# Rotary crosswise halves of q and k: plain transfers into a zeroed tile and a VectorE addition in place of adding transfers from GpSimd

## The chip, the cores and the metric

The kernel runs on one core of one Trainium2 chip. The metric is the device time of one execution in microseconds (us); lower is better. The figure for the kernel before is the median of three timed runs, 1119.79 us (1118.19 to 1121.5).

## The reference

A decoder trunk of two layers over 512 tokens of width 1024, batch 1, all in float32. Layer 0 mixes tokens by differential attention with 8 heads, layer 1 by a short gated causal convolution; each mixer is followed by an MLP with a squared ReLU (1024 to 4096 and back), and every sub-layer has an RMSNorm ahead and one behind.

The change concerns layer 0. Each head has two q vectors and two k vectors of 64 entries. The first 16 entries of each are rotated by position: with x1 the first 8, x2 the next 8, and c, s tables of cosine and sine by position,

```
rot = [x1*c - x2*s, x2*c + x1*s]        # entries 0..15; entries 16..63 pass unchanged
```

The rotated q is scaled by 1/8, scores are masked causally, each of the two softmaxes is taken, and the output of a head is (p0 - lambda*p1) @ v, normalised per head and multiplied by the output weights.

## The kernel before, in words

**Precision.** Every large product is three matmuls: a float32 operand is held as a rounded high part and the low remainder, and `mm3` (L65 to L69) adds high*high, high*low and low*high in PSUM. `split` (L197) makes the parts of a weight: ScalarE copies (L198), VectorE subtracts (L199).

**Layout.** q and k are held with features on the 128 partitions (two vectors of 64) and the 512 positions on the free axis, one head at a time. So the 8 entries that the rotation adds to another 8 lie on other partitions, and an engine that works partition by partition cannot add them; a transfer carries them over.

**Rotation (`rotate`, L372).** When a head's q or k projection is complete in PSUM (bank 0 for q, bank 1 for k), VectorE writes two products: `sw` with the sine table (L374) and `t1` with the cosine table (L376). The trace calls them sw_q, sw_k, t_q and t_k. Four transfers of 8 partitions each then add rows of `sw` into `t1` crosswise; GpSimd issues them (L380, L381), with addition in the transfer. Two deferred pieces follow: `high` (L389) has ScalarE round `t1` into `sw`'s place (L391) and SyncE issue moves of halves into a tile for q or k, four for q and two for k (`move`, L387); `low` (L396) has VectorE form the remainder (L399 for k, L401 for q) and SyncE issue two more moves.

**Order around it.** Work is written as a stream of small steps; a step of the filler stream is one `mm3` of 512 columns. A projection is 8 steps, so a rotation falls due every 8 steps and a head (q and k) every 16. `after(n, fn)` runs fn n steps later: before, `high` 3 or 4 steps after its rotation and `low` one more; for head 0 all after 2 steps. Attention of a head runs in units of 128 queries, 4 per head and 32 in all, interleaved with the filler steps at 4 steps per unit: scores (L468, L470), masked maximum (L476), exponentials (L483), mixing (L498 to L501), transposes (L508), values (L517), sums of squares (L520), the power on GpSimd (L525, L526), the norm factor and its product (L535, L537), transposes of the result (L549) and its split (L553, L554). The scores of a head come 12 steps after the rotation of its k. A planner in the framework then lays out each engine's instructions from this order and from its own estimate of when operands are ready; on the chip each engine runs its list strictly in order.

**Queues.** SyncE (SP) issues all weight loads and the moves. GpSimd issues only the rotation's transfers, between its small arithmetic (L525, L526), in order.

**Buffers.** `sw` and `t1` have two buffers each; a `t1` buffer is also what the normed output `on` (L537) takes.

**After the attention** come the rest of the output projection, the MLP of layer 0, the convolution layer and the second MLP, which the change does not touch.

Of the kernel before, what the change touches and what calls it, by code (L numbers as in the profile page):

```python
# [10 lines left out]
F32 = mybir.dt.float32  # L11
F32R = mybir.dt.float32r
AF = mybir.ActivationFunctionType
ALU = mybir.AluOpType
AX = mybir.AxisListType

P = 128
T = 512
# [23 lines left out]
def trunk(ctx: ExitStack, tc: tile.TileContext, x, xT, w_qk, w_v, w_o, w_in, w_out,  # L42
          w_up, w_down, rows, cols, lam4, rope, out):
    nc = tc.nc
    PE, ACT, DVE, POOL = nc.tensor, nc.scalar, nc.vector, nc.gpsimd
# [34 lines left out]
    def after(n, fn):  # L80
        due.append([n, fn])
# [197 lines left out]
    ap = attn.enter_context(tc.tile_pool(name="attn", bufs=2))  # L279
    ropes = ap.tile([P, 2, T], F32, name="ropes", bufs=1)  # L280

    def t512(pool, name, tag, bufs):
        return pool.tile([P, 512], F32, tag=tag, name=name, bufs=bufs)
# [83 lines left out]
    for t in q_lo:  # L367
        for c, other in ((0, slice(HD, P)), (1, slice(0, HD))):
            POOL.memset(t[other, c, :].bitcast(F32), 0.0)
    qk, oT = {}, {}  # L370

    def rotate(i, which, h, p):  # L372
        sw = t512(ap, f"sw_{which}{h}", "c", 2)
        DVE.tensor_tensor(sw, p, ropes[:, 1], op=ALU.mult)  # L374
        t1 = t512(ap, f"t1_{which}{h}", "d", 2)
        DVE.tensor_tensor(t1, p, ropes[:, 0], op=ALU.mult)  # L376

        n = HD // 8
        for c in (0, HD):
            POOL.dma_start(t1[c:c + n], sw[c + n:c + 2 * n], accum_op=ALU.add)  # L380
            POOL.dma_start(t1[c + n:c + 2 * n], sw[c:c + n], accum_op=ALU.add)  # L381
        both = ap.tile([P, 2, T], F32R, tag=which, name=f"{which}_{h}")
        hi, lo = sw.bitcast(F32R), t1.bitcast(F32R)
        top, bot = slice(0, HD), slice(HD, P)

        def move(o, a):
            nc.sync.dma_start(o.bitcast(F32), a)  # L387

        def high():  # L389

            ACT.activation(hi, t1, AF.Copy, scale=1.0 if i else -HD ** -0.5)  # L391
            for c, mine, other in ((0, top, bot), (1, bot, top)):
                for o in (mine,) if i else (mine, other):
                    move(both[o, c, :], sw[mine])

        def low():  # L396

            if i:
                DVE.tensor_tensor(lo, t1, sw, op=ALU.subtract)  # L399
            else:  # L400
                DVE.scalar_tensor_tensor(lo, t1, -HD ** -0.5, sw, op0=ALU.mult, op1=ALU.subtract)  # L401
            for c, mine, other in ((0, top, bot), (1, bot, top)):
                move(both[other, c, :] if i else q_lo[h % 2][mine, c, :], t1[mine])
            qk[which, h] = both

        for fn, n in ((high, 3 if i else 4), (low, 4 if i else 5)):
            after(n if h else 2, fn)

    def projections():

        for h in range(H):
            for i, which in enumerate("qk"):
                w = use(which, h, lead=1)
                p = banks[i]
                for kt in range(KT):
                    yield lambda: mm3(p, part(w, ALL, slice(kt * P, (kt + 1) * P)), part(hT, ALL, kt),
                                      kt == 0, kt == KT - 1)
                done(which, h)
                rotate(i, which, h, p)
# [470 lines left out]
```

## Time and profile before

| | before |
|---|---|
| timed runs, median (lowest to highest) | 1119.79 us (1118.19 to 1121.5) |
| the profiled execution, its own time | 1123.18 us |
| its span in the trace | 1121.4 us |
| TensorE (PE) busy | 1094.6 us, 98% |
| VectorE (DVE) busy | 786.1 us, 70% |
| ScalarE (ACT) busy | 534.1 us, 48% |
| GpSimd (POOL) busy | 109.6 us, 10% |
| mean granted TensorE clock | 0.994 |

All times of rows are microseconds from the start of the span unless marked ns. A busy share is that of a whole span or stretch. PEld is the load of weights into TensorE, which runs beside its matmuls; SP is SyncE, and a "q" behind an engine's name is its sequencer. A wait is the idle time of an engine just before an instruction, put down to what ended last. The projections of head 0 end at about 56 us, the attention and the filler stream with it run from there to about 235 us, and the rest of the span is the layers after it.

### The profile page before, as it was taken

To read this page: it belongs to the slowest core of one execution; us is meant where nothing else is said; L and a number is where in the kernel's file an instruction comes from. 1 tells how busy PE (TensorE), PEld (TensorE's weight loads), DVE (VectorE), ACT (ScalarE), POOL (GpSimd) and SP (SyncE) were. 2 spreads that over 40 slices of the span, in tenths; PEclk is the share of its full clock that TensorE was granted. 3 is DMA by queue.
4 is the path that set the end of the run, shared out by engine and by line. 5 is a ranking of instruction groups with operands and counts; after the bars stand their busy time and mean duration, and the time that the engine had idled before them with its cause. 6 is when DMAs were issued, how large, how long until landed. Compare 5 with 4: busy or idle time off the path is not lost.

```text
span 1121.4 us, 14617 instructions
## 1 busy us (share of the span) xinstructions
PE 1094.6 (98%) x5404; PEld 921.2 (82%) x5404; DVE 786.1 (70%) x1235; ACT 534.1 (48%) x909; POOL 109.6 (10%) x177
## 2 busy tenths in 40 slices
PE   9999999999999999999998999999999999999997
PEld 8877777779888888888888988888988888888886
DVE  6557777655979778878687544346587887797766
ACT  6536565544754554554544422225375445445532
POOL 1145554211000000000001000000000000000000
PEclk9999999999999999999998999999999999999999
DMA  8665545135134314314043323213242242143202
GB/s 307 224 155 135 139 115 132 43 130 209 38 113 150 108 44 149 132 48 159 6 145 113 114 96 101 102 40 126 82 146 65 91 151 93 58 151 106 83 19 75
DMA packets 41495, 125.88 MB, mean 112 GB/s; under 512 B 6608, under 2 KB 7248, under 8 KB 41424
## 3 DMA queue, kind: packets, MB, share of 16 engines
q1 hardware_dynamic: 39232, 123.88, 33.7%
q0 software_dynamic: 2048, 1.06, 0.8%
q8 instruction: 42, 0.69, 0.3%
q14 instruction: 29, 0.24, 0.1%
q10 hardware_dynamic: 144, 0.02, 0.0%
HBM read 111.30 MB, written 2.10 MB: 101 GB/s over the span
## 4 chain that ended last, share of the span: by engine, by line
PE 75%; DVE 4%; issue 2%; POOL 2%; DMA 2%; ACT 2%; POOLq 0%; ACTq 0%; DVEq 0%
PE bank L69 24%; PE bank L68 24%; PE bank L67 24%; DMA t_k<-sw_k 1%; DVE x_sb L616 1%; PE bank L633 1%; DMA t_q<-sw_q 1%; PE pair L67 1%; PE pair L69 1%; PE pair L68 1%; DVE mg_m L611 0%; PE bank L517 0%; DVE acc L772 0%; ACT p L483 0%; DVE hn_m L625 0%
## 5 line engine op out<-in xcount | busy, mean ns | idle before, releaser
L67 PE MATMUL bank<-hT_hi,hi_up 128*128 128x512 f32 (+1 forms) x608 | 216.5, 356 | 0.0
L69 PE MATMUL bank<-hT_hi,lo_up 128*128 128x512 f32 (+1 forms) x608 | 216.2, 356 | 0.0
L68 PE MATMUL bank<-hT_lo,hi_up 128*128 128x512 f32 (+1 forms) x608 | 216.1, 355 | 0.0
L68 PEld LDWEIGHTS bank<-hT_lo,hi_up 128*128 128x128 f32 x608 | 114.9, 189 | 16.4
L67 PEld LDWEIGHTS bank<-hT_hi,hi_up 128*128 128x128 f32 x608 | 114.9, 189 | 16.3
L69 PEld LDWEIGHTS bank<-hT_hi,lo_up 128*128 128x128 f32 x608 | 114.9, 189 | 16.1
L728 DVE TENSOR_TENSOR acc<-acc,bank 128x512 f32<-128x512 f32 x180 | 116.7, 680 | 4.4 <-PE bank L69 4.4
L198 ACT CAST hi_up<-raw_up 128x1024 fp32r<-128x1024 f32 x64 | 67.2, 1054 | 87.5 <-PE bank L69 76.4
L199 DVE TENSOR_TENSOR lo_up<-raw_up,hi_up 128x1024 fp32r<-128x1024 f32 x64 | 76.7, 1218 | 8.4 <-ACT hi_up L198 8.4
L199 DVE TENSOR_TENSOR lo_G<-rawd,hi_G 128x1024 fp32r<-128x1024 f32 x28 | 34.2, 1221 | 44.2 <-ACT hi_G L198 44.2
L68 PE MATMUL bank<-hT_lo,hi_ci 128*128 128x512 f32 (+1 forms) x176 | 62.9, 358 | 1.8 <-DVE b_m L605 1.8
L67 PE MATMUL bank<-hT_hi,hi_ci 128*128 128x512 f32 (+1 forms) x176 | 62.8, 357 | 0.9 <-ACT hT_hi L636 0.8
L69 PE MATMUL bank<-hT_hi,lo_ci 128*128 128x512 f32 (+1 forms) x176 | 62.8, 357 | 0.0
L678 ACT ACTIVATE F<-bank 128x512 f32<-128x512 f32 x64 | 37.6, 594 | 45.2 <-PE bank L69 36.0
L198 ACT CAST hi_G<-rawd 128x1024 fp32r<-128x1024 f32 x28 | 29.5, 1054 | 46.2 <-PE bank L68 31.1
L199 DVE TENSOR_TENSOR lo_E<-rawd,hi_E 128x1024 fp32r<-128x1024 f32 x28 | 34.2, 1220 | 23.6 <-ACT hi_E L198 23.6
L199 DVE TENSOR_TENSOR lo_A<-rawd,hi_A 128x1024 fp32r<-128x1024 f32 x28 | 33.5, 1220 | 19.5 <-ACT hi_A L198 19.5
L483 ACT ACTIVATE p<-pair,nm 128x128 f32<-128x128 f32 (+3 forms) x64 | 33.1, 524 | 26.9 <-DVE nm L476 24.3
L198 ACT CAST hi_E<-rawd 128x1024 fp32r<-128x1024 f32 x28 | 29.3, 1048 | 34.8 <-PE bank L68 33.6
L67 PE MATMUL bank<-hi_A,ua_hi 128*128 128x512 f32 x112 | 44.1, 393 | 0.0
L198 ACT CAST hi_A<-rawd 128x1024 fp32r<-128x1024 f32 x28 | 29.5, 1054 | 30.3 <-PE bank L68 17.7
L68 PE MATMUL bank<-lo_A,ua_hi 128*128 128x512 f32 x112 | 43.6, 390 | 0.0
(303 smaller groups left out, 2663.0 us busy)
## 6 DMA issues: line engine op xcount, KB each, us to landing
raw_up<-in_w_up SPq DMA_DIRECT2D x64, 512.0 KB, 4.2
rawd<-in_w_down SPq DMA_DIRECT2D x56, 512.0 KB, 4.4
raw_ci<-in_w_in SPq DMA_DIRECT2D x24, 512.0 KB, 3.5
raw_q<-in_w_qk SPq DMA_DIRECT2D x8, 512.0 KB, 4.9
raw_k<-in_w_qk SPq DMA_DIRECT2D x8, 512.0 KB, 4.4
q<-sw_q SPq DMA_DIRECT2D x32, 128.0 KB, 2.4
raw_wo<-in_w_o SPq DMA_DIRECT2D x8, 512.0 KB, 3.6
raw_dn<-in_w_down SPq DMA_DIRECT2D x8, 512.0 KB, 3.4
```

Of the source, the lines that this page charges most:

```text
L67: PE.matmul(o, lhsT=a[0], rhs=b[0], start=start, stop=False, skip_group_check=more)
L68: PE.matmul(o, lhsT=a[0], rhs=b[1], start=False, stop=False, skip_group_check=more)
L69: PE.matmul(o, lhsT=a[1], rhs=b[0], start=False, stop=stop, skip_group_check=more)
L198: (DVE.tensor_copy if on_dve else ACT.copy)(hi, src)
L199: DVE.tensor_tensor(lo, src, hi.bitcast(F32), op=ALU.subtract)
L483: ACT.activation(p[:, c, :w], s[:, c, :w], AF.Exp, scale=-1.0, bias=nm[:, c:c + 1], accum_out=sums[:, c:c + 1])
L616: DVE.scalar_tensor_tensor(xn, m, r, xn, op0=ALU.mult, op1=ALU.add)
L633: PE.transpose(tp[:, j * P:(j + 1) * P], hns[n][:, j * P:(j + 1) * P], ident)
L678: ACT.activation(dst, o, AF.Relu)
L728: DVE.tensor_tensor(a, a, o[t], op=op)
```

## The change

Before the loop a tile `cross` of 128 by 512 float32 is allocated once and set to zero by GpSimd. In `rotate` the four transfers become plain copies, issued by SyncE, from `sw` into the rows of `cross` that correspond to the entries 0 to 15 of each vector; all other rows of `cross` stay zero for good. A new deferred piece `turned` has VectorE add `cross` to `t1`. It runs 6 steps after the rotation, `high` 7 and `low` 8 (head 0: all after 2 steps, as before). Since there is one `cross` tile, the copies of a rotation wait until the addition of the rotation before has read it.

```
+    cross = ap.tile([P, T], F32, name="cross", bufs=1)
+    POOL.memset(cross, 0.0)
     qk, oT = {}, {}

     def rotate(i, which, h, p):
...
         for c in (0, HD):
-            POOL.dma_start(t1[c:c + n], sw[c + n:c + 2 * n], accum_op=ALU.add)
-            POOL.dma_start(t1[c + n:c + 2 * n], sw[c:c + n], accum_op=ALU.add)
+            nc.sync.dma_start(cross[c:c + n], sw[c + n:c + 2 * n])
+            nc.sync.dma_start(cross[c + n:c + 2 * n], sw[c:c + n])
...
-        for fn, n in ((high, 3 if i else 4), (low, 4 if i else 5)):
+        def turned():
+            DVE.tensor_tensor(t1, t1, cross, op=ALU.add)
+
+        for fn, n in ((turned, 6), (high, 7), (low, 8)):
             after(n if h else 2, fn)
```

## Rows read from the trace of the kernel before

**Rows 1.** The page's first part: busy time, share, instructions.

```profile
PE 1094.6 (98%) x5404; PEld 921.2 (82%) x5404; DVE 786.1 (70%) x1235; ACT 534.1 (48%) x909; POOL 109.6 (10%) x177
```

**Rows 2.** Busy time by stretch: stretch, length, busy by engine (instructions), clock, DMA share, GB/s.

```profile
62.00:215.00 153.00, 140.09 (x744) 114.70 (x743) 110.88 (x304) 82.68 (x253) 75.12 (x116) 0.99 0.51 128
215.00:235.00 20.00, 20.00 (x105) 16.64 (x105) 6.78 (x22) 6.48 (x20) 3.16 (x8) 1.00 0.16 55
```

**Rows 3.** Waits, 62 to 215: who for whom, total, times, longest.

```profile
ACT sw_q L391 <- DMA t_q<-sw_q: 7.8, 5, 5.4
DVE t_q L401 <- ACT sw_q L391: 7.8, 6, 2.7
...
DVE f L535 <- POOL f L526: 7.0, 6, 1.6
PE pair L549 <- DVE on L537: 5.2, 5, 1.6
...
PE pair L468 <- ACT p L483: 2.5, 1, 2.5
```

**Rows 4.** The chain of waits, 139 to 185: start, length, what.

```profile
152.07 0.68 DVE sw_k L374
...
155.64 4.70 DMA t_k<-sw_k
...
172.51 0.68 DVE sw_k L374
```

**Rows 5.** Timelines of POOL, DVE, PE: start, length, instruction, [idle before, releaser].

```profile
155.64 1.67 POOL L381 DMA_DIRECT2D t_k<-sw_k  x1
157.38 0.23 POOL L525 TENSOR_SCALAR f<-ss 128x1 f32<-128x1 f32 x1
...
158.29 0.16 DVE L535 TENSOR_TENSOR f<-f,rc 128x4 f32<-128x4 f32 x1 [1.47 <-POOL f L526]
...
159.68 0.63 PE L549 MATMUL pair<-ident,on 128*128 128x128 f32 x4 [1.44 <-DVE on L537]
```

**Rows 6.** Timelines of PE and ACT around three waits of TensorE.

```profile
73.84 0.47 PE L468 MATMUL pair<-k,q 128*128 128x256 f32 x2 [0.24 <-DMA k<-t_k]
...
78.40 0.63 ACT L391 ACTIVATE sw_q<-t_q 128x512 fp32r<-128x512 f32 x1 [5.39 <-DMA t_q<-sw_q]
...
79.78 0.61 PE L468 MATMUL pair<-k,q 128*128 128x384 f32 x2 [2.45 <-ACT p L483]
...
129.55 0.63 ACT L391 ACTIVATE sw_q<-t_q 128x512 fp32r<-128x512 f32 x1 [2.04 <-issue]
...
131.62 0.66 PE L508 MATMUL bank<-ident,a 128*128 128x128 f32 x4 [2.14 <-DVE a L501]
```

**Rows 7.** Busy time by stretch, after the last of these waits (clock third from last).

```profile
132.00:134.00 2.00, 2.00 (x11) 1.69 (x10) 2.00 (x9) 1.29 (x5) 0.00 (x0) 0.67 0.87 203
134.00:136.00 2.00, 2.00 (x9) 1.81 (x9) 1.82 (x4) 0.94 (x5) 1.80 (x4) 0.50 0.60 127
```

**Rows 8.** Timeline of DVE: a remainder of k and the instruction behind it.

```profile
161.34 0.69 DVE L399 TENSOR_TENSOR t_k<-t_k,sw_k 128x512 fp32r<-128x512 f32 x1
161.95 0.74 DVE L554 SCALAR_TENSOR_TENSOR oT_lo<-pair,g_sub,oT_hi 128x512 fp32r<-128x512 f32 x1
```

**Rows 9.** SyncE: timeline of moves, then landing of q's transfers, then the k loads.

```profile
171.89 2.39 SPq L387 DMA_DIRECT2D q<-sw_q  x4
174.46 1.10 SPq L387 DMA_DIRECT2D q_lo<-t_q  x2
...
DMA to landing us min/median/max: 2.2/2.4/3.8
...
raw_k<-in_w_qk SPq DMA_DIRECT2D x8, 512.0 KB, 4.4
```

**Rows 10.** Timeline of POOL: zeroing at the start and the next work.

```profile
1.89 0.52 POOL L369 MEMSET q_lo<- 64x512 f32 x1
...
33.87 1.04 POOL L74 TENSOR_TENSOR r<-r,mhalf 128x4 f32<-128x4 f32 x1 [29.50 <-DVE r L73]
```

## The prediction

> **What bounds the kernel now.** I read the page's busy times first. TensorE is busy 1094.6 us of 1121.4 [rows 1], so a change elsewhere can only win back its idle time. The table of stretches says where that idle time is. From 62 to 215 us, where the rotations run beside the attention, TensorE is busy 140.09 of 153.00 us, so it idles 12.91 us; from 215 to 235 us, when the last rotation is done, it idles nowhere [rows 2]. 12.91 us is what this stage has to give.
>
> The chain of waits says what the stage waits for. From 139 us to the last rotation it hardly touches TensorE: it runs from VectorE's `sw` and `t1` through GpSimd's issue and the landing of the adding transfer to ScalarE's `high`, VectorE's `low` and the next `sw`. From one `sw_k` to the next it takes 172.51 - 152.07 = 20.44 us, and 4.70 us of it is one transfer of t_k underway [rows 4]. At 16 steps per head a step is 20.44 / 16 = 1.28 us.
>
> The timelines tell how this reaches TensorE, in two ways.
>
> First, through GpSimd. The last adding transfer of t_k was issued at 155.64 us and held GpSimd's sequence for 1.67 us; the small factor `f` behind it started only at 157.38, VectorE stood 1.47 us for it, and TensorE 1.44 us for the `on` that VectorE made with it [rows 5]. In the list of waits this is 7.0 us of VectorE in 6 waits, and 5.2 us of TensorE in 5 waits for `on` [rows 3].
>
> Second, through ScalarE. `high` stands in ScalarE's queue until its transfer has landed, and exponentials are queued behind it. At 78.40 us ScalarE had stood 5.39 us for t_q, and TensorE stood 2.45 us for the exponentials that came next; at 129.55 `high` was late again, VectorE's `low` waited for it with a mixing product queued behind, and TensorE stood 2.14 us for that product [rows 6]. In sum ScalarE stood 7.8 us for t_q, and VectorE's `low` of q as long for ScalarE [rows 3]. After the 2.14 us wait the granted clock was 0.67 and then 0.50, its lower level of 1.2 GHz, for two stretches of 2 us each [rows 7]; that costs (0.33 + 0.50) x 2 = 1.7 us.
>
> **The change part by part.** Removed: 64 issues on GpSimd, and with them both ways above. TensorE's waits for `on` (5.2), for the exponentials (2.5) and for the product (2.1) come to 9.8 of the 12.91 us, and with the clock's 1.7 us the gross gain is 11.5 us. `f` is then late only if the sum of squares on ScalarE is; ScalarE meets `high` when the data has been added for a step already.
>
> Added on VectorE: 16 additions of 128x512. No row shows this addition; the nearest is L399, also two SBUF operands of that size, 0.69 us long, with the next instruction starting 0.61 us behind it [rows 8]. 16 x 0.61 = 9.8 us of VectorE, or 16 x 0.69 = 11.0 by whole durations. VectorE is busy 110.88 of 153.00 us there [rows 2], so it has room, and it loses waits of 7.0 + 7.8 = 14.8 us. It becomes no bound, but its order is strict: the addition of k falls 6 steps, 7.3 us, after `sw_k`, which is where `f` and `on` are made: VectorE took up `f` 158.29 - 152.07 = 6.2 us after `sw_k`, and TensorE had `on` after 159.68 - 152.07 = 7.6 [rows 4, 5]. I charge half of these 8 additions to TensorE: 8 x 0.61 / 2 = 2.4 us. If all 16 were on the path it would be 9.8, if none, nothing.
>
> Added on SyncE: 64 issues. The moves of q cost 2.39 / 4 = 0.60 us each, the low ones 1.10 / 2 = 0.55 [rows 9]; the new ones have 8 partitions where these have 64, so 0.60 is the upper end, and nothing the lower. At 0.55 four are 2.2 us a rotation. The landing behind it is 2.2 to 3.8 us, 2.4 in the median, for moves on the same queue [rows 9]. For q, SyncE has just the two low moves of k ahead: 0.6 (`sw`) + 0.5 + 2.2 + 2.4 = 5.7 us after `sw_q` starts. For k it has the four and two moves of q ahead, 3.5 us from the end of `high`. With the gain a step is some 1.22 us; `high` starts one step ahead of `sw_k` and takes 0.63 [rows 6], so it ends 0.6 us ahead, and k lands at 3.5 - 0.6 + 2.2 + 2.4 = 7.5 us. The addition stands 6 steps, 7.3 us, behind `sw`: q lands 1.6 us early, k 0.2 us late. 8 x 0.2 = 1.6 us, of which I charge 1 us to TensorE; with a load in front, 3.8 - 2.4 = 1.4 us more for every k, it would be 8 x 1.6 = 13, and with SyncE free ahead of k nothing.
>
> The later `high` and `low`: the low moves of k now are issued behind step 8 and the two high ones, at about 11.5 us after `sw_k`, and land by 13.9; the scores stand 12 steps, 14.6 us, behind. That is covered by 0.7 us, and costs 1 us a head where it isn't.
>
> The first head: its pieces all come after 2 steps, its first scores waited 0.24 us for k already [rows 6]. A plain transfer lands 4.70 - 2.4 = 2.3 us sooner than the adding one [rows 4, 9], and the addition takes 0.6 of it: 1.7 us sooner if k's copies go ahead of q's six moves on SyncE, 3.5 - 1.7 = 1.8 us later behind them. I take 0.7 us, nearer to the second, since q's moves are written first.
>
> The zeroing of `cross` is twice the 0.52 us of half a tile, and GpSimd idles 29.50 us before its next work [rows 10]: nothing.
>
> **The sum.** -11.5 + 2.4 + 1.0 + 0.7 = -7.4, taken as -7 us. For the profiled execution, 1123.18 us, that is 1116; against the median of the timed runs, 3.4 us lower, 1119.79 - 7 = 1113 us.
>
> **A rule that speaks against it.** The row shows moves of SyncE landing within 3.8 us though 512 KB loads, 4.4 us in the median, share their queue [rows 9]. The Trainium skill, "DMA: Bandwidth & Descriptors", section "Queues, rings and completion order", says that each DMA engine takes the descriptors of one queue row in ring order, while different rows take turns. So a crosswise copy just behind a weight load on SyncE's row would wait for it, where GpSimd's row took turns. No row shows how often that will be; it is the mechanism of the slower rival below.
>
> **The rivals.**
> *Slower: VectorE waits for the copies.* Before, only ScalarE stood for a transfer; now VectorE does, with masks, mixing and weight remainders behind it. For: the k copies have hardly any margin. Against: the rows of landing, and that SyncE's six moves of q are 3.5 us of a head's 20. If each rotation's copies land 2.5 us later than worked out, behind loads and moves, q waits 0.9 us and k 2.7, 3.6 a head and 29 us in all; with two thirds of it reaching TensorE, -11.5 + 3.1 + 19 = +11, and with fewer such rotations less: I put the case at +5, 1125 us. It decides from a mean wait of about 0.8 us a rotation (16 x 0.8 x 2/3 = 8.4).
> *No change: the gaps close up and open elsewhere.* `on` also hangs on ScalarE's exponentials and squares, and the additions delay VectorE. If half of the gross gain comes, -5.7 + 4.1 = -1.6: 1118 us. A step that shrinks until k is late for the scores ends here too (7 heads x 1 us against 7).
> *More: all idle time goes.* 12.91 + 1.7 less 3 us of costs: -11.5, 1108 us. For it: nothing else in the stage is busier than VectorE's 72%. Against: the small waits for transposed products remain.
> *The order changes.* The planner lays out each engine anew; that can move TensorE's waits by a few us either way and is spread over the cases.
>
> **How the numbers follow.** Forecast (-4 to -10 us, 1110 to 1116): 0.45. More: 0.13. No change: 0.22. Slower: 0.20. A measurement can tell 0.3%, 3.4 us, from no change: faster 0.58, same 0.22, slower 0.20. The range that leaves out about a tenth on either side goes from 1106 to 1125.
>
> **What would show it.** Right: no wait of VectorE's L535 for GpSimd over 0.5 us, no ScalarE wait for a transfer at `high`, TensorE's idle time from 62 us to the last rotation down to about 6 us, the head's period at about 19.5 us, no stretch at 0.5 clock there. Wrong: waits of the new addition for the copies over 0.5 us in most heads, or scores waiting for k's low moves; the same idle time of TensorE under other names would be the second rival.

## The result, and the profile after

The changed kernel takes 1145.56 us (median; 1144.9 to 1147.31) against 1119.47 us (1118.19 to 1121.5) before: a ratio of 1.0234, interval 1.0214 to 1.0254, which is 26.2 us (24.0 to 28.4) slower where 7 us faster was forecast. Its profiled execution took 1144.9 us, with a span of 1143.1 us, 21.7 longer than that of before; that one lay 3.7 us above its median, so some 4 us of the difference don't show in the pair of traces.

First the page's busy times of the changed kernel.

```profile
PE 1103.3 (97%) x5404; PEld 926.0 (81%) x5404; DVE 798.0 (70%) x1251; ACT 534.1 (47%) x909; POOL 57.7 (5%) x114
```

Against [rows 1], TensorE runs the same 5404 instructions in 8.7 us more, and idles 1143.1 - 1103.3 = 39.8 us where it idled 26.8: 13.0 us more. The two make up the whole 21.7 us. VectorE's 16 additions are its 1251 - 1235 instructions more, and at 0.69 us each 11.0 of the 11.9 us more; GpSimd is rid of half its work. The stretches of the changed kernel (length, busy by engine, clock, DMA share, GB/s) say where it happened.

```profile
62.00:215.00 153.00, 135.25 (x672) 108.98 (x671) 110.03 (x282) 73.35 (x219) 22.95 (x48) 0.96 0.46 121
215.00:235.00 20.00, 13.86 (x64) 11.42 (x64) 10.53 (x34) 8.34 (x29) 3.66 (x8) 0.83 0.25 56
```

Beside [rows 2], TensorE's idle time is 17.75 us where it was 12.91, and 6.14 us where it was nothing, since the rotations now last past 215 us. The clock is 0.96 and 0.83 where it was 0.99 and 1.00; (0.99 - 0.96) x 153 + (1.00 - 0.83) x 20 = 8.0 us, most of the 8.7 us of longer matmuls. VectorE and ScalarE are busy for less of the stage than before: neither is the bound.

Next VectorE's and then SyncE's timeline of the changed kernel, one head of it (start, length, line, instruction).

```profile
137.85 0.69 DVE L376 TENSOR_TENSOR sw_k<-bank,ropes 128x512 f32<-128x512 f32 x1 [0.18 <-DMA k<-sw_k]
...
142.41 0.69 DVE L409 TENSOR_TENSOR t_q<-t_q,cross 128x512 f32<-128x512 f32 x1
...
149.72 0.69 DVE L376 TENSOR_TENSOR sw_q<-bank,ropes 128x512 f32<-128x512 f32 x1
...
153.96 0.68 DVE L409 TENSOR_TENSOR t_k<-t_k,cross 128x512 f32<-128x512 f32 x1
...
164.88 0.69 DVE L409 TENSOR_TENSOR t_q<-t_q,cross 128x512 f32<-128x512 f32 x1
```

```profile
143.13 0.64 SPq L382 DMA_DIRECT2D cross<-sw_k  x1
143.98 2.66 SPq L389 DMA_DIRECT2D q<-sw_q  x4
146.75 1.17 SPq L389 DMA_DIRECT2D q_lo<-t_q  x2
147.97 0.68 SPq L383 DMA_DIRECT2D cross<-sw_k  x1
148.71 0.68 SPq L382 DMA_DIRECT2D cross<-sw_k  x1
149.43 0.62 SPq L383 DMA_DIRECT2D cross<-sw_k  x1
...
154.66 0.65 SPq L382 DMA_DIRECT2D cross<-sw_q  x1
155.40 1.17 SPq L389 DMA_DIRECT2D k<-sw_k  x2
156.66 1.19 SPq L389 DMA_DIRECT2D k<-t_k  x2
157.90 0.68 SPq L383 DMA_DIRECT2D cross<-sw_q  x1
158.62 0.68 SPq L382 DMA_DIRECT2D cross<-sw_q  x1
159.34 0.62 SPq L383 DMA_DIRECT2D cross<-sw_q  x1
```

Read the two together. `sw_k` is done at 138.54, but its first copy is issued only at 143.13, at the moment the addition of q (142.41 to 143.10) has read `cross`: there is one `cross`, and k must not overwrite what q has not yet read. Behind this copy SyncE's order has q's six moves, and the other three copies of k only behind those. The last is out at 150.05; VectorE adds k at 153.96. At 154.66, 0.02 us after that addition, the first copy of q goes, though `sw_q` was done at 150.41; k's four moves stand ahead of the other three, and so on to the next addition of q. That is a closed loop of addition, copies, landing, addition, and it went round in 164.88 - 142.41 = 22.5 us. From the first copy's issue to the start of the last one's SyncE takes 149.43 - 143.13 = 6.3 us of it for k and 159.34 - 154.66 = 4.7 us for q. The two landings, which count from the start of an issue, are not recorded here; at 2.3 us each, an estimate from the plain copies shown at the end, they are 4.6, the two additions 1.4, and the 5.5 us left over go by while VectorE is at what its order has ahead of the additions. So on the chip the loop is not closed tightly. Of the 15 rotations that follow another, 13 have their first copy issued within 0.1 us of the end of the addition before.

The waits of SyncE in the changed kernel, 62 to 215 us (who for whom, total, times, longest), have the same at their head.

```profile
SPq L382 <- DVE rho L504: 25.1, 6, 5.7
SPq L382 <- DVE t_k L409: 9.7, 4, 4.7
SPq L382 <- DVE t_q L409: 5.4, 1, 5.4
```

L382 is the first copy. The addition, L409, is named in 5 of these 11 waits; the `rho` named in the others is what VectorE starts just behind it, here at 143.22. In these three rows SyncE stood 40.2 us. The waits of the other engines, which answer to [rows 3], show little of this.

```profile
PE pair L554 <- DVE on L542: 7.4, 3, 2.8
...
DVE sw_k L376 <- DMA k<-sw_k: 5.6, 4, 2.4
...
DVE f L540 <- POOL f L531: 5.2, 6, 1.8
...
ACT sw_k L393 <- DVE t_k L409: 2.4, 2, 1.8
...
DVE t_k L409 <- DMA cross<-sw_k: 1.1, 1, 1.1
```

ScalarE stands for no transfer any more at `high`, and VectorE stood for a copy once, for 1.1 us. VectorE's order, laid out ahead, has the additions where the copies will have landed; what is late stands late in the order, and the list of waits does not tell it. The timelines do: for the last six heads TensorE had done 8 to 15 steps of the stream (the matmuls of L67 to L69, three to a step) from `sw_k` to the addition of k, where 6 are written, and 5 to 9 in the kernel with the copies on GpSimd below.

One wait of VectorE has grown. Its `sw_k` stood 5.6 us in 4 waits for the moves of the `sw_k` before it to land (0.2 us once in the kernel before), since the two share a buffer of `sw`. Here the chain of waits passes through the loop (start, length, what).

```profile
93.67 0.70 DVE t_k L409
...
94.38 0.64 SPq L382
...
95.12 0.52 SPq L389
...
95.69 2.29 DMA k<-sw_k
...
98.10 0.69 DVE sw_k L376
```

The landing is counted from 95.69, where the issue of the second move begins. A late addition makes `high` and its moves late, and these hold back the next head's rotation. That is one way from the loop to the head's period. From 62 to 225 us this is the only place where the chain names a copy into `cross`; elsewhere it runs mostly through matmuls, masks and exponentials in their order. So the traces show the loop, and the runs below what opening it is worth; how its lateness is passed on to TensorE is only in part shown.

### The profile page after: what moved, and what is told of

Same layout as the page of the kernel before. It is cut to its first block, busy times and chain, and to the rows that moved or that the text cites. A ratio compares the mean times of both kernels' runs of the same rounds, so it can differ in the third digit from the quotient of the medians.

```text
span 1143.1 us, 14558 instructions
## 1 busy us (share of the span) xinstructions
PE 1103.3 (97%) x5404; PEld 926.0 (81%) x5404; DVE 798.0 (70%) x1251; ACT 534.1 (47%) x909; POOL 57.7 (5%) x114
## 4 chain that ended last, share of the span: by engine, by line
PE 79%; DVE 6%; issue 2%; ACT 2%; POOL 1%; DMA 1%; SPq 0%; POOLq 0%; DVEq 0%; ACTq 0%
PE bank L67 25%; PE bank L68 25%; PE bank L69 24%; PE bank L522 1%; DVE x_sb L621 1%; PE bank L638 1%; DVE pair L481 1%; PE pair L473 1%; PE pair L475 1%; PE bank L513 1%; ACT p L488 1%; PE pair L69 1%; PE pair L67 0%; PE pair L68 0%; DMA raw_ci<-in_w_in 0%
## 5 line engine op out<-in xcount | busy, mean ns | idle before, releaser
L67 PE MATMUL bank<-hT_hi,hi_up 128*128 128x512 f32 (+1 forms) x608 | 216.5, 356 | 0.0
L69 PE MATMUL bank<-hT_hi,lo_up 128*128 128x512 f32 (+1 forms) x608 | 216.2, 356 | 0.0
L67 PEld LDWEIGHTS bank<-hT_hi,hi_up 128*128 128x128 f32 x608 | 114.8, 189 | 16.3
L69 PEld LDWEIGHTS bank<-hT_hi,lo_up 128*128 128x128 f32 x608 | 114.8, 189 | 16.3
L67 PE MATMUL bank<-hT_hi,hi_ci 128*128 128x512 f32 (+1 forms) x176 | 62.5, 355 | 0.9 <-ACT hT_hi L641 0.8
L69 PE MATMUL bank<-hT_hi,lo_ci 128*128 128x512 f32 (+1 forms) x176 | 62.4, 355 | 0.0
L199 DVE TENSOR_TENSOR lo_A<-rawd,hi_A 128x1024 fp32r<-128x1024 f32 x28 | 33.5, 1220 | 19.5 <-ACT hi_A L198 19.5
L67 PE MATMUL bank<-hi_A,ua_hi 128*128 128x512 f32 x112 | 44.1, 393 | 0.0
L67 PE MATMUL bank<-hi_E,ub_hi 128*128 128x512 f32 x112 | 43.6, 389 | 0.0
```

Of the source, the lines that this page charges most:

```text
L67: PE.matmul(o, lhsT=a[0], rhs=b[0], start=start, stop=False, skip_group_check=more)
L69: PE.matmul(o, lhsT=a[1], rhs=b[0], start=False, stop=stop, skip_group_check=more)
L199: DVE.tensor_tensor(lo, src, hi.bitcast(F32), op=ALU.subtract)
```

## The experiments

The theories: that the single tile and SyncE's order close a loop (the tile); that the loss comes from t1 held longer in its ring of two buffers, which `on` shares (the ring); that it is the later `high` and `low` (the positions); that it is VectorE's addition; that it is SyncE as the issuer. Each ratio below is to the kernel before, timed on the same chip, with its 95% interval. The planner lays out every edited kernel anew, so no run holds the order fixed, and none tells the chip's own times from the planner's estimate of them as what sets the loop's pace.

**Two tiles.** The two tiles need room: `ones`, which is read early, shares the buffer of `sq`.

```
-    cross = ap.tile([P, T], F32, name="cross", bufs=1)
+    crosses = [ap.tile([P, T], F32, name=f"cross{n}", bufs=1) for n in range(2)]
...
     def rotate(i, which, h, p):
+        cross = crosses[i]
```

> The changed kernel with two cross tiles, one for q and one for k (a 128x128 scratch tile shares a buffer with the table of ones to make room). Theory B: copies of a rotation no longer wait for the addition of the one before, go out as soon as sw is there, and the period falls from about 22.7 to under 21 us, 1120 to 1132 us. Theory A: the positions are the same, 1140 to 1147 us. Theory C: 1143 to 1148 us.

Measured: 1119.83 us, 0.9978 (0.9963 to 0.9992). The loss is gone: 1.0234 - 0.9978 is 2.6%, 29 us. SyncE's timeline of this kernel shows a part of how.

```profile
164.35 0.65 SPq L384 DMA_DIRECT2D cross<-sw_k  x1
165.05 0.62 SPq L385 DMA_DIRECT2D cross<-sw_k  x1
165.72 0.62 SPq L384 DMA_DIRECT2D cross<-sw_k  x1
166.91 2.43 SPq L391 DMA_DIRECT2D q<-sw_q  x4
```

Its `sw_k` ran from 163.63 to 164.32, so the first copy follows at once, and three are out before the moves of q. It is not so in every head: at 133.63 the first copy of k follows q's six moves, 5.5 us after the end of its `sw_k`. But no copy of k has to wait for the addition of q any more, nor one of q for that of k. VectorE's timelines, first of the changed kernel and then of the one with two tiles, have the `sw_k` of the fourth head and of the last; over the four heads between, a head takes (204.87 - 116.53) / 4 = 22.1 us with one tile and (181.80 - 112.01) / 4 = 17.4 with two.

```profile
116.53 0.69 DVE L376 TENSOR_TENSOR sw_k<-bank,ropes 128x512 f32<-128x512 f32 x1
...
204.87 0.69 DVE L376 TENSOR_TENSOR sw_k<-bank,ropes 128x512 f32<-128x512 f32 x1 [0.92 <-DMA k<-sw_k]
```

```profile
112.01 0.68 DVE L378 TENSOR_TENSOR sw_k<-bank,ropes 128x512 f32<-128x512 f32 x1
...
181.80 0.69 DVE L378 TENSOR_TENSOR sw_k<-bank,ropes 128x512 f32<-128x512 f32 x1 [0.22 <-PE bank L69]
```

**One tile, copies on another queue; and moves on another queue.** Either edit leaves the wait for the tile and takes the moves out from behind it.

```
-            nc.sync.dma_start(cross[c:c + n], sw[c + n:c + 2 * n])
+            POOL.dma_start(cross[c:c + n], sw[c + n:c + 2 * n])
...
```

> The changed kernel with its copies issued by GpSimd instead of SyncE, still plain, still one cross tile, same positions. Theory D, the issues on SyncE and their place behind the moves: 1120 to 1130 us, copies issued within 3 us of one another. Theory B by the tile alone (each rotation's copies wait for the last addition): 1130 to 1143 us. Theory A: 1140 to 1150 us.

```
         def move(o, a):
-            nc.sync.dma_start(o.bitcast(F32), a)
+            POOL.dma_start(o.bitcast(F32), a)
```

> The changed kernel (1145.6 us) with its copies left on SyncE and one cross tile, but the moves of high and low issued by GpSimd. Theory B1, the one tile costs because the copies' wait for the last addition and the moves stand in one queue: the loop of copies, addition, moves, copies is broken, 1108 to 1124 us. Theory B2, the wait for the one tile costs on any queue that issues at SyncE's pace: 1138 to 1150 us.

Measured: 1112.11 us, 0.9917 (0.9896 to 0.9939), with the copies on GpSimd, and 1115.07 us, 0.994 (0.9921 to 0.996), with the moves there. So the single tile alone is no harm, and SyncE as the issuer of copies alone is none; the loss needs both in one order. With the copies on GpSimd the wait for the tile is still there, as the waits of its GpSimd, 62 to 215 us, show.

```profile
POOL f L530 <- ACT sq L525: 57.0, 24, 4.5
...
POOL cross L382 <- DVE t_q L409: 10.5, 2, 6.6
```

10.5 us it stood for the addition of q, but behind it stood only `f` and the next copies, and VectorE's wait for `f` came to 3.8 us. With two tiles and GpSimd (both edits above):

> Two cross tiles and the copies issued by GpSimd. With one tile on GpSimd it was 1112.1 us. Theory B2: the wait for the tile still costs there, 1103 to 1109 us. Theory B1: on GpSimd the wait holds up nothing but the small factor, 1109 to 1114 us.

Measured: 1119.01 us, 0.997 (0.9952 to 0.9987), slower than with one tile, and within the intervals the same as two tiles with the copies on SyncE (0.9978): with two tiles the queue makes no clear difference. Why the second tile costs here, no run tells. The traces differ in that VectorE stood 5.9 us in 4 waits at its additions for the copies, where with one tile it stood 0.5 us in 2, and TensorE 4.0 us in 3 waits for mixing products, for which it has no wait listed with one tile.

**The positions.** Three pairs: the changed kernel and the one with copies on GpSimd, with the three pieces at the early places; and the kernel before with its pieces at the late ones.

```
-        for fn, n in ((turned, 6), (high, 7), (low, 8)):
+        for fn, n in ((turned, 2 if i else 3), (high, 3 if i else 4), (low, 4 if i else 5)):
```

> The changed kernel (1145.6 us) with the addition, high and low written at steps 2/3/4 (k) and 3/4/5 (q) behind the rotation in place of 6/7/8. Theory A, the late written positions hold the t1 buffers too long and starve `on` and the next t1: back to 1120 to 1128 us, period of a head near 20 us. Theory B, the four copies wait on SyncE for the addition before (one cross tile) and stand behind the moves: VectorE then waits in its own queue for the copies instead, 1138 to 1155 us. Theory C, the 16 additions on VectorE by themselves: 1143 to 1148 us, no change.

> Copies on GpSimd, one tile, with the addition, high and low at steps 2/3/4 and 3/4/5. If the later positions are what keeps VectorE and ScalarE from standing for the copies: 1116 to 1125 us; if positions don't matter as in the two pairs before: 1110 to 1114 us.

```
-        for fn, n in ((high, 3 if i else 4), (low, 4 if i else 5)):
+        for fn, n in ((high, 7), (low, 8)):
```

> The kernel before (adding transfers from GpSimd, no cross tile) with only high and low moved from 3/4 and 4/5 to 7 and 8 steps. Theory A: most of the loss comes with the positions alone, 1135 to 1150 us, and t1 is held about 3 us longer. Theories B, C and D: nothing that they blame is there; ScalarE's wait for the adding transfer goes and the time is 1113 to 1123 us.

Measured: 1.0226 (1.0202 to 1.025), beside 1.0234; 0.9915 (0.9892 to 0.9938), beside 0.9917; 0.9997 (0.9982 to 1.0011). The written positions change nothing, with a loop or without one. But they hardly reach the chip: TensorE's steps from `sw_k` to the addition of k, head by head, are 14, 12, 8, 15, 12, 13, 14, 9 in the changed kernel and 14, 12, 8, 15, 12, 14, 14, 8 with the early places, and in the kernel before `low` of k comes 7 steps behind `sw_k` in the last three heads with either. So the pairs rule out the writing as the cause; what it costs to run the pieces later, they do not tell. ScalarE's wait for the adding transfer of q, which was expected to go in the kernel before with late places, was 8.2 us there beside 7.8 [rows 3].

**The addition.** Once added to the kernel before, ahead of `high`, with a tile that stays zero; once taken out of the two kernels that copy.

```
+        def turned():
+            DVE.tensor_tensor(t1, t1, cross, op=ALU.add)
+
-        for fn, n in ((high, 3 if i else 4), (low, 4 if i else 5)):
+        for fn, n in ((turned, 3 if i else 4), (high, 3 if i else 4), (low, 4 if i else 5)):
```

> The kernel before with one VectorE instruction more per rotation, the addition of a tile of zeros to t1 just ahead of high, 16 in all, adding transfers and positions as before. It prices the addition alone: 2.4 us by the prediction, so 1120 to 1125 us; up to 1131 if every one of the 16 stands on the path; 1120 or less if it falls into waits.

```
-        for fn, n in ((turned, 6), (high, 7), (low, 8)):
+        for fn, n in ((high, 7), (low, 8)):
```

> The changed kernel (1145.6 us) without the addition of cross to t1, so that q and k lack the crosswise terms; the 64 copies still go from SyncE into the one tile, and nothing reads it. Theory B1, the loss is the copies' wait for the addition in SyncE's queue: without it 1108 to 1120 us, although SyncE issues just as much. Theory D, the 64 issues on SyncE themselves: 1135 us or more.

> The same left out (no addition) with the copies on GpSimd, 1112.1 us with the addition. It prices the addition and the wait for its copies where the copies are early: 1104 to 1110 us if the addition costs there what it cost in the kernel before (8 us), 1110 to 1113 if it is hidden.

Measured: 1130.47 us, 1.0069 (1.0045 to 1.0093), so 7.7 us (5.0 to 10.4) for 16 additions in the kernel before; 1121.12 us, 0.9986 (0.9972 to 1.0), without the addition on SyncE; 1107.6 us, 0.9867 (0.9843 to 0.9892), without it on GpSimd, which makes the addition worth 0.9917 - 0.9867 = 0.5%, 5.6 us, there (some 2 to 9 with both intervals). In the kernel before with the addition, VectorE stands for the transfers, and ScalarE's `high` for the addition.

```profile
ACT sw_k L393 <- DVE t_k L409: 15.3, 7, 4.3
...
DVE t_k L409 <- DMA t_k<-sw_k: 8.4, 6, 3.7
```

On SyncE the addition's removal is worth 1.0234 - 0.9986 = 2.5%, five times what it is on GpSimd: what went there is not the 0.69 us of work but the reader that the next copies wait for. SyncE's order is still the one shown above, a copy, six moves, three copies, as its timeline has it.

```profile
143.22 0.69 SPq L382 DMA_DIRECT2D cross<-sw_k  x1
144.02 2.43 SPq L389 DMA_DIRECT2D q<-sw_q  x4
146.58 2.44 SPq L389 DMA_DIRECT2D q_lo<-t_q  x2
149.38 0.70 SPq L383 DMA_DIRECT2D cross<-sw_k  x1
150.13 0.67 SPq L382 DMA_DIRECT2D cross<-sw_k  x1
150.85 0.62 SPq L383 DMA_DIRECT2D cross<-sw_k  x1
```

So this order alone, with nothing waiting for the copies, does no harm beside before. Yet it is 1.2%, 13 us, behind its fellow with the copies on GpSimd (0.9867). With two tiles the two queues are alike (0.9978 and 0.997), so the price of copies beside moves without a loop is not one number, and what it consists of is open.

**The ring.** `on` gets a buffer of its own (and `ones` shares that of `sq`, as above), in the changed kernel and in the one with copies on GpSimd.

```
-        on = t512(ap, f"on_{u}", "d", 2)
+        on = t512(ap, f"on_{u}", "on", 1)
```

> The changed kernel with the normed output `on` in a buffer of its own, so that it and t1 no longer take turns. Theory R, the late pieces reach TensorE by that ring (t1 held until its last move has landed, `on` waits for it, TensorE waits for `on`, and the next t1 for `on`): 1125 to 1140 us. If they reach TensorE by q and k themselves or by the banks: 1142 to 1149 us.

> Copies on GpSimd, one tile, positions 6/7/8, and `on` in a buffer of its own. If the shared ring of t1 and `on` still makes TensorE wait there: 1104 to 1110 us; if not: 1110 to 1114 us.

Measured: 1146.66 us, 1.0218 (1.0196 to 1.0239), for the first. TensorE's 7.4 us for `on` are gone from its waits, and others stand in their place.

```profile
PE bank L67 <- DVE t_k L378: 6.0, 5, 1.6
...
PE pair L473 <- DMA k<-t_k: 5.2, 4, 2.6
```

Taking away one wait gave it another name while the loop was there; that `on` shares the ring is not the cause. Without the loop the same edit is worth something: 1108.8 us, 0.9869 (0.985 to 0.9888) beside 0.9917, the fastest kernel of the study that leaves no work out: 0.9869 is 1.3%, 15 us, below before on its chip, where the change is 26 above. Its TensorE idles little in the stage.

```profile
62.00:215.00 153.00, 150.24 (x820) 125.14 (x819) 124.34 (x338) 88.86 (x271) 58.83 (x124) 1.00 0.49 128
```

2.76 us idle where it was 12.91 [rows 2], at the full clock.

## Why the prediction was wrong

**The stage and the gross gain: the size near, the way not shown.** The 12.91 us of idle time and the clock's loss were to be had: the kernel with plain copies on GpSimd and without the addition is 14.9 us faster (11.5 were forecast), and TensorE in it idles 153.00 - 151.08 = 1.92 us of the stage. But taking the 64 issues from GpSimd was not needed for it, for that kernel still has them there. VectorE's wait for `f`, the first of the two ways, is 4.7 us in it, and 8.1 us in the kernel without the addition where GpSimd issues nothing, beside 7.0 before [rows 3]. TensorE's wait for `on`, 5.2 us before, is 0.3 us in the one and not listed in the other. Whether the shorter landings, the shorter issues or the new order did that, no run tells apart.

**The addition: mis-sized within its bounds.** 2.4 us were charged between 0 and 9.8; it cost 5.6 us in one kernel and 7.7 in another. Half of k's additions was too little: all 8 of them at 0.69 us are 5.5 us, so either those of q count too or waits come with them; no run splits them.

**SyncE: the step that failed.** "k lands at 3.5 - 0.6 + 2.2 + 2.4 = 7.5 us. The addition stands 6 steps, 7.3 us, behind `sw`: q lands 1.6 us early, k 0.2 us late." In the head shown the last copy of k was issued 150.05 - 137.85 = 12.2 us after `sw_k` started and the addition came at 16.1. The working counted what stands ahead of the copies on SyncE and the landing, as if they were free to go when `sw_k` was there. They were not: 143.13 - 138.54 = 4.6 us went by until the addition of q had read the tile. The section on the change names this wait; the working has no term for it. And the wait is fed by itself, since a late addition of k holds the copies of q, and these the next addition of q; 1 us was charged for what the edits that open the loop put at 22 to 35. The 6 steps did not hold either, as the counts above show. The four issues were also put between 0 and 0.60 us each and taken at 0.55; they start 0.72 apart. And the sum has the last issue twice, since a landing counts from the start of its issue; without that, k would have been some 0.3 us early by the same working.

**The first head: too little.** 0.7 us were taken, from -1.7 to 1.8; the first score of head 0 began at 77.20 instead of 73.84 [rows 6], 3.4 us later: three of k's copies stood behind q's moves there, and the addition of k waited 1.1 us for them. The zeroing cost nothing, as was said; the whole tile took 0.52 us, no more than half a tile had [rows 10].

**The signs named in advance.** ScalarE's waits at `high` went, as was said. VectorE's waits for `f` did not fall below 0.5 us: 5.2 us in 6 remain, up to 1.8, with a GpSimd that issues nothing; GpSimd itself stood 148.5 us in 24 waits for ScalarE's sums of squares, from 62 to 215 us, and that `f` is late when these are was the prediction's own condition. The head's period was to be 19.5 us and was 22.1 over the last four.

**The rivals.** The slower one had the sign, by another mechanism: VectorE was to stand for the copies in most heads, and did so once. Its full size, 11 us, was short of 26 as well, because it took a copy's lateness to end with its rotation. Of order in the DMA engines' rings, the rule weighed there, no run tells anything by itself; the loss can be told without it, since it goes when the second tile comes, with all transfers still issued by SyncE.

**The sum again.** Removed, -14.9 us; the addition, 5.6; the copies with one tile on SyncE rather than on GpSimd, 1.0234 - 0.9917 = 3.2%, 35.5 us: 26.2, as measured. That is a walk from kernel to kernel, so its sum closes by itself; what it tells is the size of the steps. How much of the 35.5 us is the loop depends on the edit that opens it: 29 by the second tile, 33 by the moves on GpSimd (1.0234 - 0.994), 22 by leaving the addition out, with its 5.6 us taken off. By each of them it is the largest step. With the copies on GpSimd the time would have been in the range of the forecast, -9.3 us (-11.6 to -6.8), but by other terms: -14.9 and 5.6 in place of -11.5 and 4.1, and with the issues left on GpSimd.

## What to carry to other kernels

A transfer into a single buffer waits for the buffer's last reader; write down which queue issues it and what stands behind it there, for all of that waits too. Where the reader in turn depends on the transfers behind, the waits close to a loop, and its length (issue, landing and reading of every user of the buffer, once round; here 17.0 of 22.5 us) has to be set beside the period, with room for what the order puts between, not the first pass with its margin. When an order is laid out ahead, such a loop shows in the issuing engine's own waits and in the distance of like instructions, not in the waits of the busy engines; a second buffer or a second queue opens it.

## What the runs showed of the hardware

A copy of 8 partitions costs SyncE no less than a move of 64: in the changed kernel the issues of the copies (line, engine, operation, count, min/median/max ns, from when to when) have medians of 0.64 to 0.67 us, one group shown here, and those of the moves 0.54 to 0.59.

```profile
L382 SPq DMA_DIRECT2D cross<-sw_q x16: 624/668/782, 56.4 to 204.9; - x16
```

The same plain copies took GpSimd 0.52 us in the median (0.52 to 0.75), where the adding ones had taken medians of 0.95 to 1.26, and land sooner than the adding ones from the same queue: median us from issue to landing is the last column, first before, then with plain copies on GpSimd.

```profile
t_q<-sw_q POOLq DMA_DIRECT2D x32, 16.0 KB, 3.7
...
t_k<-sw_k POOLq DMA_DIRECT2D x32, 16.0 KB, 3.6
```

```profile
cross<-sw_q POOLq DMA_DIRECT2D x32, 16.0 KB, 2.3
cross<-sw_k POOLq DMA_DIRECT2D x32, 16.0 KB, 2.6
```

Between these two kernels the addition in the transfer is 1.0 to 1.4 us of landing, more than the 0.69 us that VectorE's addition lasts.
